# A one-core encoder layer: the residual's squares in the up product, the first v products on unscaled x, and other buffers for the last output pieces

## The chip, the cores and the metric

The kernel runs on one core of a Trainium2 chip. The core has five engines with queues of their own: TensorE (PE, matrix products into PSUM banks, with PEld its weight loads), VectorE (DVE), ScalarE (ACT), GpSimd (POOL) and SyncE (SP), which here issues the DMAs. An engine works through its queue in order; semaphores order the engines among each other.

The metric is the device time of one execution in microseconds (us); the median of several runs is given. One execution was also profiled: the profile has its own time and a span, from the first to the last instruction that it shows.

## The reference

One layer of an encoder on x of 2048 tokens by 1024 features, all in float32:

```
xn = rms_norm(x, mix_norm_g)
aq,ak,av,mq,mk,mv,mo,i,f,ga,gm = split(xn @ w_in)
A  = chunked band attention(aq, ak, av)      # own 64-token chunk and 8 before it
M  = gated recurrence with matrix memory(conv(mq), conv(mk), mv, i, f), normed, times sigmoid(mo)
y  = sigmoid(ga) * (A @ w_att_proj) + sigmoid(gm) * (M @ w_mlstm_proj)
x  = x + y @ w_out                           # the residual stream, called x2 below
x  = x + relu(rms_norm(x, ffn_norm_g) @ w_up)^2 @ w_down
out = rms_norm(x, final_norm_g)
rms_norm(x, g) = x * (mean(x*x over features) + 1e-6)^-0.5 * g
```

Since the norm's factor is one number per token, it can be applied to a product's rows after the product, where the token is the output's partition or column.

## The kernel before, in words

**Precision and tiles.** Each float32 operand is split into a high part (ACT, a cast) and a low part (DVE, source minus high); a product is three matmuls, high·high, high·low and low·high. `split_now` (L367, L369) does so for a weight tile of 128x1024, `split` (L703, or L705 with a scale, and L708, or L710) for a 128x512 tile of activations. Weight tiles come through four buffers `wraw` (512 KB loads) and three split buffers `wsp`. Activations lie feature by token: eight tiles k of 128 features by 512 tokens for a block of 512 tokens. Further pools: 28 split tiles `r`, 16 `ctx`, 6 `tmp`, 4 `sc` (mostly for reloads), 2 `bias`, and 8 PSUM banks.

**Stages.** Four blocks b of 512 tokens, in two halves s of two blocks. For each block: the norm (`norm_in`, `square_in`, `scale_in`), then with the split tiles `xs` the products v (`token_tiles`, L428 to L430), the i and f gates (L536), mv, then five feature tiles for each of four head groups, then ga, the attention and recurrence beside them, and the two projections. After two blocks, for the half as a whole: the gm product (2 quads), the out product (2), the up product (8) and the down product (8). A quad (`quad`, L511) is a 2x2 block product done with seven products, whose sums and differences DVE forms (`combine`, L1310; `spread`, L1364 to L1373; in the out product L1444).

**The first norm.** For block 0, `square_in` loads each x tile (L669), squares it on ACT (L675) and adds it up on DVE (L679). Products with ones (L633) give the mean by token, DVE and POOL (L644, the power −0.5) the factor `r_x`, PE broadcasts it (L652), `scale_in` multiplies x by gain and factor (L692), stores it and splits it into `xs`.

**The residual's squares.** When the out product has finished a tile of x2, `x2_tile` stores it to DRAM, multiplies it by the up norm's gain on ACT (L1471) and squares it on ACT (L1478, L1482); POOL adds the squares up (L1485) in the two `bias` buffers. `norm_mid` takes the sums by products with ones (L1506); its factor is only used later, in the down product.

**The end.** `final1` squares each finished tile (L1667), adds it up (L1670) and multiplies it by the last gain (L1674). `final_scale` takes the sums (L1684), POOL the power (L1693). `final_out` transposes on PE (L1702), scales on ACT (L1709) or DVE (L1711) into a `tmp` buffer and sends it out (L1715).

**Order.** Nothing is scheduled on the chip. Each part is a Python generator that says which engine it uses and for how long, in the author's estimate; `Flow` runs them against each other and writes each engine's instructions in the order that comes out. So a change anywhere can move instructions elsewhere, by the estimated times and by when buffers come free. `dense` is the main thread with all large products; it and its calls set PE's order.

Of the kernel before, what the change touches and what calls it, by code (L numbers as in the profile page):

```python
# [27 lines left out]
P = 128  # L28
# [17 lines left out]
N_Q = N_G + N_O + 2 * N_F  # L46

# [157 lines left out]
class Layer:  # L205
# [48 lines left out]
    def setup(self):  # L254
        nc, io = self.nc, self.io
        nc.vector.memset(self.half, -0.5)
        nc.vector.memset(self.ones, 1.0)
        yield "sp", 700
        nc.sync.dma_start(self.const, io["consts"].rearrange("p (a b) -> p a b", a=2))
        yield "sp", 50  # L260
        nc.sync.dma_start(self.gcol, io["gcol"].rearrange("p (a b) -> p a b", a=3))

    def setup_late(self):
        nc, io, fl = self.nc, self.io, self.fl
        (raw,) = yield "get", self.temp, 1
# [32 lines left out]
    def loader(self):  # L298
        fl, io = self.fl, self.io
        i = 0  # L300
        for s in range(NS):
            for n in range(2 * N_W):
                (raw,) = yield "get", self.wraw, 1
                fl.spawn(self.split_w(i, io["w"][n % N_W], raw), 0)
                i += 1
# [43 lines left out]
    def split_w(self, i, src, raw):  # L349
        yield "sp", 1750, 2000  # L350
        self.nc.sync.dma_start(raw, src)
        yield from self.split_now(i, raw)
# [165 lines left out]
    def dense(self):  # L518
        fl = self.fl
        none = [None] * KT  # L520
        for b in range(NB):
            s, B = b // 2, self.blk[b]
            xe = B["xn"]
# [5 lines left out]
            yield from self.token_tiles(xs, xe, lambda t, bk: self.evac_v(b, t, bk))  # L529
# [3 lines left out]
            for k in range(KT):  # L533
                yield "pe", 433
                for j in range(2):
                    self.nc.tensor.matmul(bk[:40], self.gw[:, k], xs[k][:, j],  # L536
                                          start=k == 0 and j == 0, stop=k == KT - 1 and j == 1)
            fl.spawn(self.gates(b, bk), 1)
            yield from self.token_tiles(xs, none, lambda t, bk: self.evac_mv(b, t, bk))
            self.banks.want = 2  # L540
            for j in range(4):
                for fn in (self.evac_q, self.evac_k, self.evac_conv_q, self.evac_conv_k, self.evac_og):
                    (bk,) = yield from self.feature_tile(xs, none)
# [32 lines left out]
            self.tots = yield "get", self.bias, 2  # L576
# [24 lines left out]
    def norm_in(self, b):  # L601
# [4 lines left out]
        if b == 0:  # L606
            (tot,) = yield "get", self.ctx, 1
            for k in range(KT):
                (x,) = yield "get", self.ctx, 1
                xt.append(x)  # L610
                fl.spawn(self.square_in(b, k, x, tot, ev), 0)
# [32 lines left out]
        nc.gpsimd.tensor_tensor(r, r, self.half, op=ALU.pow)  # L644
        if b % 2 == 1:
# [9 lines left out]
        for k in range(KT):  # L655
            (dst,) = yield "get", self.rpool, 1
            B["xs"].append(dst)
            if b > 0:
                (x,) = yield "get", self.sc, 1
                xt.append(x)  # L660
            fl.spawn(self.scale_in(b, k, xt[k], bk, dst, done[k]), 2)
        fl.set(B["xs_ev"])
# [3 lines left out]
    def square_in(self, b, k, x, tot, ev):  # L666
        fl, nc = self.fl, self.nc
        yield "sp", 900, 2000
        nc.sync.dma_start(x[:, :T], self.io["xt"][b, k])  # L669
        if k > 0:  # L670
# [12 lines left out]
    def scale_in(self, b, k, slot, bk, dst, ev):  # L683
# [12 lines left out]
        fl.set(self.blk[b]["xn"][k])  # L696
# [17 lines left out]
    def attention(self, b):  # L714
# [5 lines left out]
        B["kq"] = {}  # L720
        for j in range(4):
# [22 lines left out]
    def evac_v(self, b, t, bk):  # L744
# [4 lines left out]
        yield "act", act_ns(512, True)  # L749
        nc.scalar.copy(v[:, :, 0], src)  # L750
        yield "dve", dve_ns(512)
        nc.vector.tensor_sub(v[:, :, 1], src, v[:, :, 0].bitcast(F32))
# [201 lines left out]
    def gates(self, b, bk):  # L954
# [11 lines left out]
        yield "dve", 85  # L966
        V.tensor_add(self.gf, bk[:, :32].rearrange("p (a b) -> p a b", a=NT), self.bif)
# [103 lines left out]
    def evac_mv(self, b, t, bk):  # L1071
# [5 lines left out]
        yield "act", act_ns(512, True)  # L1077
        nc.scalar.copy(mv[:, :, 0:128], bk.rearrange("p (h c) -> p h c", h=MH))
# [384 lines left out]
    def x2_tile(self, s, h, j, x, ht, w, hev):  # L1463
# [10 lines left out]
        tot = self.tots[h][:, :512]  # L1474
        if not B["sums"]:
# [363 lines left out]
```

## Time and profile before

| | us |
|---|---|
| median of 3 runs (2904.01 to 2909.32) | 2906.3 |
| the profiled execution | 2907.77 |
| its span | 2906.0 |
| PE busy | 2853.2 (98%) |
| DVE busy | 2069.0 (71%) |
| ACT busy | 1562.5 (54%) |
| POOL busy | 98.4 (3%) |

PE's granted clock was 0.998 of full speed. The span divides, by PE's own lines, roughly into: the first half's blocks to 660 us, its gm and out products to 830, its up product to 1140, its down product to 1450, and the same for the second half, with the tail from 2890 on.

How to read it: a group or timeline row names the line of the code, the engine and the operation, output<-input by tile names without buffer numbers, and how many. In the timeline the first two numbers are start and length in us; what stands in brackets is how long the engine was idle before, and what ended that wait. PE is a matmul, PEld its weight load, SPq a DMA issue on SP's queue. A row of the waits says which engine and line waited for which, in total, how often, and the longest.

### The profile page before, as it was taken

What the parts mean: (1) busy time and instruction counts of PE and PEld (TensorE: products, weight loads), DVE (VectorE), ACT (ScalarE), POOL (GpSimd) and SP (SyncE); (2) the same over time, 40 slices, a digit from 0 to 9 for tenths busy, and PEclk for the clock granted to TensorE, in tenths of its full rate; (3) what the DMA queues carried; (4) which work ended last, traced back from release to release, by engine and by line L of the source; (5) the groups of instructions that cost most, each with busy time, mean ns of one, the idle gap of its engine ahead of it and who ended that gap; (6) DMA issues with size and microseconds to landing.
All of it is one profiled execution on the core that took longest, in us unless ns stands there. A gap on an engine that the chain in (4) does not pass through costs nothing.

```text
span 2906.0 us, 39057 instructions
## 1 busy us (share of the span) xinstructions
PE 2853.2 (98%) x13760; PEld 2381.8 (82%) x13760; DVE 2069.0 (71%) x3797; ACT 1562.5 (54%) x2708; POOL 98.4 (3%) x152
## 2 busy tenths in 40 slices
PE   7999999999999999999999999999999999999998
PEld 6888878888778888888888888888887788888887
DVE  5786569876885557898748864697769744468775
ACT  3664356654565556444536653566555655564444
POOL 0000000000110000000000000000001100000000
PEclk9999999999999999999999999999999999999999
DMA  5326942258875558766543246222588655587652
GB/s 200 101 91 235 331 143 94 73 180 282 276 246 212 210 203 290 255 227 209 203 157 105 87 130 212 97 82 68 176 290 288 221 200 186 191 288 232 201 183 88
DMA packets 232902, 548.07 MB, mean 189 GB/s; under 512 B 26240, under 2 KB 32512, under 8 KB 232704
## 3 DMA queue, kind: packets, MB, share of 16 engines
q1 hardware_dynamic: 232704, 545.57, 55.9%
q8 instruction: 108, 1.77, 0.2%
q14 instruction: 90, 0.74, 0.1%
HBM read 375.60 MB, written 169.87 MB: 188 GB/s over the span
## 4 chain that ended last, share of the span: by engine, by line
PE 58%; DVE 7%; DMA 4%; issue 2%; ACT 2%; SPq 0%; POOL 0%; POOLq 0%; DVEq 0%; ACTq 0%
PE bank L511 38%; PE bank L428 5%; PE bank L429 5%; PE bank L430 5%; DMA sc<-u 2%; DVE wsp L369 1%; DVE r L708 1%; PE bank L878 1%; PE bank L944 1%; PE bank L913 1%; DVE sc L919 1%; ACT wsp L367 0%; ACT r L703 0%; DMA sc<-hn 0%; DVE ctx L1108 0%
## 5 line engine op out<-in xcount | busy, mean ns | idle before, releaser
L511 PE MATMUL bank<-r,wsp 128*128 128x512 f32 x6720 | 1537.6, 390 | 15.2 <-DVE ctx L1444 5.4
L511 PEld LDWEIGHTS bank<-r,wsp 128*128 128x128 f32 x6720 | 1259.2, 188 | 283.3 <-ACT r L703 6.8
L369 DVE TENSOR_TENSOR wsp<-wraw,wsp 128x1024 fp32r<-128x1024 f32 x456 | 557.7, 1223 | 306.1 <-ACT wsp L367 301.8
L367 ACT CAST wsp<-wraw 128x1024 fp32r<-128x1024 f32 x456 | 478.9, 1050 | 534.6 <-PE bank L511 295.4
L428 PE MATMUL bank<-r,wsp 128*128 128x512 f32 x1152 | 463.3, 402 | 3.4 <-DVE tmp L890 2.0
L430 PE MATMUL bank<-r,wsp 128*128 128x512 f32 x1152 | 450.2, 391 | 0.0
L429 PE MATMUL bank<-r,wsp 128*128 128x512 f32 x1152 | 449.8, 390 | 0.0
L703 ACT CAST r<-sc 128x512 fp32r<-128x512 f32 x276 | 170.0, 621 | 162.7 <-DMA sc<-u 71.3
L430 PEld LDWEIGHTS bank<-r,wsp 128*128 128x128 f32 x1152 | 216.2, 188 | 47.0
L428 PEld LDWEIGHTS bank<-r,wsp 128*128 128x128 f32 x1152 | 216.9, 188 | 42.5 <-DVE tmp L890 2.8
L429 PEld LDWEIGHTS bank<-r,wsp 128*128 128x128 f32 x1152 | 217.1, 188 | 36.7
L708 DVE TENSOR_TENSOR r<-sc,r 128x512 fp32r<-128x512 f32 x276 | 187.8, 700 | 58.9 <-ACT r L703 58.3
L1619 DVE TENSOR_TENSOR ctx<-bank,ctx 128x512 f32<-128x512 f32 x192 | 132.1, 689 | 73.6 <-PE bank L511 73.3
L1310 DVE TENSOR_TENSOR ctx<-bank,ctx 128x512 f32<-128x512 f32 x120 | 82.7, 689 | 85.6 <-PE bank L511 85.6
L928 ACT ACTIVATE sc<-sc,scs 128x640 f32<-128x640 f32 (+4 forms) x128 | 97.3, 761 | 82.3 <-DVE scs L925 78.3
L919 DVE CUSTOM_DVE_ANT_0 sc<-bank,bias 128x320 f32<-128x320 f32 (+3 forms) x240 | 103.1, 462 | 18.8 <-PE bank L913 18.1
L878 PEld LDWEIGHTS bank<-r,r 128*128 128x128 f32 x672 | 98.3, 189 | 12.4 <-DVE r L949 2.9
L878 PE MATMUL bank<-r,r 128*128 128x256 f32 (+1 forms) x672 | 105.5, 279 | 1.9 <-DVE r L949 1.2
L1554 ACT ACTIVATE ctx<-ctx 128x512 f32<-128x512 f32 x96 | 60.6, 632 | 85.5 <-DVE ctx L1310 85.4
L428 PE MATMUL bank<-wsp,r 128*128 128x512 f32 x256 | 102.5, 400 | 1.5 <-ACT r L703 1.5
L429 PE MATMUL bank<-wsp,r 128*128 128x512 f32 x256 | 100.5, 393 | 0.0
L430 PE MATMUL bank<-wsp,r 128*128 128x512 f32 x256 | 99.4, 391 | 0.0
(214 smaller groups left out, 2925.7 us busy)
## 6 DMA issues: line engine op xcount, KB each, us to landing
wraw<-in_w SPq DMA_DIRECT2D x176, 512.0 KB, 3.5
wraw<-in_wf SPq DMA_DIRECT2D x136, 512.0 KB, 4.3
sc<-u SPq DMA_DIRECT2D x224, 256.0 KB, 3.6
wraw<-wsum SPq DMA_DIRECT2D x96, 512.0 KB, 3.9
wsum<-wraw SPq DMA_DIRECT2D x64, 512.0 KB, 2.9
u<-ctx SPq DMA_DIRECT2D x128, 256.0 KB, 2.4
u<-tmp SPq DMA_DIRECT2D x96, 256.0 KB, 2.7
tmp<-proj SPq DMA_DIRECT2D x64, 256.0 KB, 4.5
```

The source lines that it names most:

```text
L367: nc.scalar.copy(w[:, 0], raw)
L369: nc.vector.tensor_sub(w[:, 1], raw, w[:, 0].bitcast(F32))
L428: mm(ps, lh, rh, start=first, stop=False)
L429: mm(ps, lh, rl, start=False, stop=False)
L430: mm(ps, ll, rh, start=False, stop=last)
L511: mm(ps, wv[:, x, k, n], a[:, y], start=new and k == 0 and x == y == 0, stop=k == 3 and x == 1, skip_group_check=True)
L703: self.nc.scalar.copy(dst[:, 0], src)
L708: self.nc.vector.tensor_sub(dst[:, 1], src, dst[:, 0].bitcast(F32))
L878: nc.tensor.matmul(bk[:, c0:c0 + w], st, sl[:, x, o:o + w], start=n == 0, stop=n == total - 1)
L919: nc.vector.tensor_tensor_reduce(out=e[:, x * w:x * w + w], in0=bks[x][:, :w], in1=br[:, j0 + x * w:j0 + x * w + w], op0=ALU.add, op1=ALU. ...
L928: nc.scalar.activation(e[:, :n], e[:, :n], AF.Exp, scale=-1.0, bias=mx, accum_out=st[:, 2:3])
L1619: nc.vector.tensor_add(a, ps, a)
```

## The change

1. **First block.** `square_in` now also multiplies each x tile by the gain alone and splits it (lines 695 and 697 of the changed file: ACT the high part, DVE the low), into eight tiles `xg`. v, the gates and mv of block 0 are taken from `xg`; the factor `r_x` is applied where their banks are emptied: `evac_v`, `evac_mv` by the scale operand, `gates` in four rows with the bias. `xs` (with the factor) is still made, for the other feature tiles. The DMAs are put in a written order: gcol, then x tiles and weight tiles in turn, then the constants, the last x tiles, and the small loads.
2. **Squares of x2.** `x2_tile` no longer squares. `norm_mid` is started with the third quad of the up product (and `norm_in` of the next block with it); it loads x2 again into `sc` buffers, squares on ACT and adds on DVE, in the new function `square_mid`.
3. **The end.** In the second half, the square of the last tile (3, 1) isn't added up: it is multiplied by ones in products of its own, into the bank that holds the others' sums. The output pieces of the last block go into `sc` and `wraw` buffers in place of `tmp`.

The core of the diff:

```diff
+LAST = (3, 1)
 def setup(self):
-        yield "sp", 700
-        nc.sync.dma_start(self.const, ...)
         yield "sp", 50
         nc.sync.dma_start(self.gcol, ...)
+        self.fl.set(self.ev_gain)
+        yield "wait", [self.w_sent[2]]
+        yield "sp", 700, 2000
+        nc.sync.dma_start(self.const, ...)
+        self.fl.set(self.ev_const)
 def setup_late(self):
+        yield "wait", [self.x_sent[6], self.ev_const]
 def loader(self):
+                first = s == 0 and n < KT // 2
+                if first:
+                    yield "wait", [self.x_sent[2 * n]]
...
 def dense(self):
             xs = B["xs"]
-            yield from self.token_tiles(xs, xe, ...evac_v...)
+            vs = xs if b > 0 else B["xg"]
+            yield from self.token_tiles(vs, B["xn"], ...evac_v...)
...
-            yield from self.token_tiles(xs, none, ...evac_mv...)
+            yield from self.token_tiles(vs, none, ...evac_mv...)
+            if b == 0:
+                fl.put(self.rpool, *vs)
...
-            self.tots = yield "get", self.bias, 2
...
-            for h in range(2):
-                fl.spawn(self.norm_mid(s, h), 2)
-            if b + 1 < NB:
-                fl.spawn(self.norm_in(b + 1), 3)
             for i in range(N_F):
+                if i == 2:
+                    for h in range(2):
+                        fl.spawn(self.norm_mid(s, h), 3)
+                    if b + 1 < NB:
+                        fl.spawn(self.norm_in(b + 1), 3)
 def square_in(self, b, k, x, tot, ev):
+        dst, g = self.blk[b]["xg"][k], self.gcol[:, 0, k:k + 1]
+        if k > 0:
+            yield "wait", [self.w_sent[(k - 1) // 2]]
         nc.sync.dma_start(x[:, :T], self.io["xt"][b, k])
+        fl.set(self.x_sent[k])
+        yield "wait", [self.ev_gain]
+        nc.scalar.mul(dst[:, 0], x[:, :T], g)
+        nc.vector.scalar_tensor_tensor(dst[:, 1], x[:, :T], g, dst[:, 0].bitcast(F32), op0=ALU.mult,
+                                       op1=ALU.subtract)
+        fl.set(self.blk[b]["xn"][k])
 def evac_v(self, b, t, bk):
+        if b == 0:
+            r = self.rr["x"][:, t:t + 1]
+            yield "wait", [self.ev_r]
+            nc.scalar.mul(v[:, :, 0], src, r)
+            nc.vector.scalar_tensor_tensor(v[:, :, 1], src, r, v[:, :, 0].bitcast(F32), ...)
...
 def x2_tile(...):
-        tot = self.tots[h][:, :512]
-        if not B["sums"]:
-            nc.scalar.square(tot, x5)
-        else:
-            nc.scalar.square(sq[:, :512], x5)
-            nc.gpsimd.tensor_tensor(tot, tot, sq[:, :512], op=ALU.add)
 def norm_mid(self, s, h):
+        for j in range(KT):
+            (x,) = yield "get", self.sc, 1
+            fl.spawn(self.square_mid(s, h, j, x, tot[:, :512], summed), 3)
+        yield "wait", summed
...
+    def square_mid(self, s, h, j, x, tot, summed):
+        x5 = x[0][:, :512]
+        yield "sp", 900, 2000
+        self.nc.sync.dma_start(x5, self.x2d[2 * s + h].ap()[j])
+        yield "act", act_ns(512)
+        self.nc.scalar.square(tot if j == 0 else x5, x5)
+        if j > 0:
+            yield "wait", [summed[j - 1]]
+            yield "dve", dve_ns(512)
+            self.nc.vector.tensor_add(tot, tot, x5)
+        self.fl.put(self.sc, x)
+        self.fl.set(summed[j])
 def final1(...):
+        if s == NS - 1 and (j, h) == LAST:
+            (self.sq_last,) = yield "get", self.temp, 1
+            nc.scalar.square(self.sq_last[:, :512], a)
+            fl.set(self.last_ev)
+            nc.scalar.mul(a, a, self.gcol[:, 2, j:j + 1])
+            return
 def final_scale(...):
+        if last:
+            yield "wait", [self.last_ev]
+            for t in range(NT):
+                nc.tensor.matmul(bk[:, 2 * t:2 * t + 2], self.sq_last[:, t * P:(t + 1) * P], self.ones,
+                                 start=False, stop=True, skip_group_check=True)
 def final_out(...):
+        pool = self.temp
+        if s == NS - 1 and h == LAST[1]:
+            pool = (self.sc, self.wraw)[g]
```

More of the change, by code (lines that the diff above doesn't have):

```diff
@@ L347, in load_w, with split_w @@
         self.fl.set(ev)
-    def split_w(self, i, src, raw):
+    def split_w(self, i, src, raw, sent=None):
         yield "sp", 1750, 2000
         self.nc.sync.dma_start(raw, src)
+        if sent is not None:
+            self.fl.set(sent)
         yield from self.split_now(i, raw)
@@ L528, in dense @@
             xs = B["xs"]
-            yield from self.token_tiles(xs, xe, lambda t, bk: self.evac_v(b, t, bk))
+            vs = xs if b > 0 else B["xg"]
+            yield from self.token_tiles(vs, B["xn"], lambda t, bk: self.evac_v(b, t, bk))
             yield "wait", [self.ev_late]
@@ L720, in attention @@
         B["kq"] = {}
+        if b == 0:
+            yield "wait", [self.ev_late]
         for j in range(4):
@@ L965, in gates @@
                              start=True, stop=True)
-        yield "dve", 85
-        V.tensor_add(self.gf, bk[:, :32].rearrange("p (a b) -> p a b", a=NT), self.bif)
+        if b == 0:
+            for c in range(NT):
+                yield "dve", 85
+                V.scalar_tensor_tensor(self.gf[:, c], bk[:, c * 8:c * 8 + 8], self.rr["x"][:, c:c + 1],
+                                       self.bif[:, c], op0=ALU.mult, op1=ALU.add)
+        else:
+            yield "dve", 85
+            V.tensor_add(self.gf, bk[:, :32].rearrange("p (a b) -> p a b", a=NT), self.bif)
         fl.put(self.temp, tmp)
@@ L1680, in final_scale @@
         (bk,) = yield "get", self.banks, 1
-        yield "wait", summed
+        last = s == NS - 1 and h == LAST[1]
+        yield "wait", [e for j, e in enumerate(summed) if not last or j != LAST[0]]
         yield "pe", 900
```

84 lines of the change are left out of this document (50 added, 34 removed).

## The prediction

> **What bounds the kernel now.** I read the page's busy line and chain first, then who made TensorE (PE) wait, then the timeline at the places where it waited.
>
> ```profile
> PE 2853.2 (98%) x13760; PEld 2381.8 (82%) x13760; DVE 2069.0 (71%) x3797; ACT 1562.5 (54%) x2708; POOL 98.4 (3%) x152
> PE 58%; DVE 7%; DMA 4%; issue 2%; ACT 2%; SPq 0%; POOL 0%; POOLq 0%; DVEq 0%; ACTq 0%
> ```
>
> PE is busy 2853.2 of 2906.0 us, so 52.8 us are idle. The change takes no product away, so all it can win lies in those 52.8 us. The waits of PE, longest first:
>
> ```profile
> PE bank L633 <- DVE ctx L679: 11.3, 1, 11.3
> PE bank L511 <- DVE ctx L1444: 5.4, 3, 2.1
> PE bank L511 <- ACT r L705: 3.7, 2, 1.9
> ...
> PE bank L652 <- POOL r_x L644: 2.3, 1, 2.3
> ...
> PE bank L511 <- DVE r L708: 1.3, 1, 1.3
> ...
> PE bank L1506 <- POOL bias L1485: 1.1, 2, 0.8
> ```
>
> The columns are total, times and longest, in us. Three places carry them: the first block's norm (L633, L652) at the start, the out product and its neighbours (L1444, L705, L708, L1485), and the tail. The change touches all three. In the built program's order of instructions PE, DVE and ACT differ from before only around these places; elsewhere their rows follow each other as they did, so I take the other waits (attention, the down product) as unchanged.
>
> **Part 1, the start.** The timeline of before (start, length, engine, line):
>
> ```profile
> 0.73 1.28 ACT L675 ACT_TABLE_LOAD   x1 [0.73 <-PEq L1829]
> ...
> 0.73 3.71 SPq L669 DMA_DIRECT2D ctx<-in_xt  x8
> ...
> 3.45 0.63 ACT L675 ACTIVATE ctx<-ctx 128x512 f32<-128x512 f32 x1 [1.44 <-DMA ctx<-in_xt]
> ...
> 5.88 3.34 ACT L675 ACTIVATE tmp<-ctx 128x512 f32<-128x512 f32 x5 [1.09 <-DMA ctx<-in_xt]
> ...
> 11.06 1.04 ACT L367 CAST wsp<-wraw 128x1024 fp32r<-128x1024 f32 x1 [1.04 <-DMA wraw<-in_w]
> ...
> 13.25 1.23 DVE L369 TENSOR_TENSOR wsp<-wraw,wsp 128x1024 fp32r<-128x1024 f32 x1
> 13.41 1.94 POOL L644 TENSOR_TENSOR r_x<-r_x,half 128x4 f32<-128x4 f32 x1 [12.48 <-DVE r_x L640]
> ...
> 15.41 2.07 PE L652 MATMUL bank<-const,r_x 128*128 128x128 f32 x8 [2.27 <-POOL r_x L644]
> ...
> 18.97 0.80 PE L428 MATMUL bank<-wsp,r 128*128 128x512 f32 x1 [1.49 <-ACT r L703]
> ...
> 825.26 0.95 PE L1506 MATMUL bank<-ones,bias 128*128 128x2 f32 x8
> ...
> 2894.54 0.72 ACT L1674 ACTIVATE ctx<-ctx,gcol 128x512 f32<-128x512 f32 x1
> ```
>
> The first product starts at 18.97, after eight x tiles, the sum of squares, the power on POOL, the broadcast on PE, and a scaled split. Changed, its inputs are one x tile times the gain, and one weight tile. I walk the new chain:
> - SP issues one DMA per 3.71/8 = 0.46 us. gcol now stands first, so x tile 0, which was ready at 3.45, comes at about 3.9.
> - In the built program ACT waits for that tile's DMA ahead of its table load, because the wait became an instruction of its own. The load, hidden at 0.73 before, ends at 3.9 + 1.28 = 5.2.
> - The gain product (0.72, the L1674 row) ends at 5.9, the tile's square (0.63) at 6.5.
> - Weight tile 0 is now second in the queue. Tiles x0 to x2 are as many bytes as x0 and this weight tile; they were in at 5.88. With gcol ahead that is 6.3, so ACT is the later one. Its high half (1.04) ends at 7.6.
>
> So the first product starts at 7.65, 11.3 us earlier. Three things come off. PE issues two products and then needs the weight's low half on DVE (1.23 behind 7.6, so 8.9), a wait of 0.4. The norm's sixteen PE rows, which ran before the first product, now stand inside the stream; the L1506 row gives 0.95 for eight at full clock, some 1.3 for all beyond what overlaps. The slow first products (0.80 for the first) are paid in both. Start: 11.3 − 0.4 − 1.3 = 9.6.
>
> What must hide behind the stream: the norm chain, moved and not removed. The last x tile is now issued behind five weight tiles and five small loads. Eight x tiles came from 3.45 to 9.2, 0.8 us each, so with the bytes of 17 tiles ahead it lands at 3.9 + 17 × 0.8 = 17.5 or a little later; its split stands behind that of a weight tile on ACT and DVE, and I place it at 25. It is needed when the fourth weight tile starts, three tiles of 24 products (0.22 each by the stage row of part 2) and the slow start after 8, at 26. The power (1.94) then has some 7 us of PE work before the broadcast asks for it. Scaling and splitting eight tiles moves beside the first block's mv product, 96 products or 21 us long, with DVE nearly full there. The gate recurrence stands behind these eight tiles on DVE, and PE's small products on it may wait 0 to 0.5 us. The scalings in evac_v, evac_mv and gates replace copies one for one, four gate rows replace one, all behind PE's stream. On SP the eight xn stores wait for the later scaling and two weight tiles stand behind some of them; these are used three query or key tiles later, so I cost that at nothing, and at a wait of some 2 us if the scaling slips. Bounds: 11.3 − 1.3 = 10 with no wait for the low half, and 8.2 if the table load costs all of 0.73 to 3.45 (see the rivals). I take 9.6.
>
> **Part 2, the squares of the residual stream.**
>
> ```profile
> 754.62 2.00 POOL L1485 TENSOR_TENSOR bias<-bias,tmp 128x512 f32<-128x512 f32 x1 [166.35 <-ACT tmp L1482]
> 756.65 0.69 DVE L1364 TENSOR_TENSOR tmp<-ctx,ctx 128x512 f32<-128x512 f32 x1 [1.18 <-POOL bias L1485]
> ...
> 758.06 2.53 PE L511 MATMUL bank<-r,wsp 128*128 128x512 f32 x8 [1.77 <-ACT r L705]
> ...
> 816.61 2.98 PE L511 MATMUL bank<-r,wsp 128*128 128x512 f32 x12 [1.78 <-DVE ctx L1444]
> 821.04 4.38 PE L511 MATMUL bank<-r,wsp 128*128 128x512 f32 x18 [1.45 <-DVE ctx L1444]
> ...
> 825.54 1.77 DVE L1364 TENSOR_TENSOR tmp<-ctx,ctx 128x512 f32<-128x512 f32 x1
> ...
> 842.57 3.74 PE L511 MATMUL bank<-r,wsp 128*128 128x512 f32 x15 [1.28 <-DVE r L708]
> ...
> 2204.47 2.41 DVE L710 SCALAR_TENSOR_TENSOR r<-tmp,r 128x512 fp32r<-128x512 f32 x2
> 2205.04 1.29 POOL L1485 TENSOR_TENSOR bias<-bias,tmp 128x512 f32<-128x512 f32 x1 [160.79 <-ACT tmp L1482]
> ...
> 2208.19 4.18 PE L511 MATMUL bank<-r,wsp 128*128 128x512 f32 x17 [1.89 <-ACT r L705]
> ...
> 2265.54 7.18 PE L511 MATMUL bank<-r,wsp 128*128 128x512 f32 x30 [2.15 <-DVE ctx L1444]
> ```
>
> ```profile
> L1485 POOL TENSOR_TENSOR bias<-bias,tmp x28: 1285/1444/1998, 754.6 to 2277.8; 128x512 f32<-128x512 f32 x28
> 880.00:920.00 40.00, 40.00 (x182) 33.29 (x181) 22.37 (x26) 20.80 (x30) 1.97 (x1) 1.00 0.63 222
> sc<-u SPq DMA_DIRECT2D x224, 256.0 KB, 3.6
> ```
>
> (The first line is one source line's instructions, min/median/max in ns. The second is a stage: length, then busy PE, PEld, DVE, ACT, POOL, the clock, DMA share, GB/s. The third is from the page's DMA issues.)
>
> These rows show more than POOL's own wait. While POOL adds, DVE stands still: L1364 takes 0.69 at 756.65 and 1.77 at 825.54, two L710 take 2.41 where two take some 1.3, and at 756.65 DVE is held 1.18 until POOL ends. So each of the 28 adds costs DVE some 1.1 us where DVE is what PE waits for. Removed: 28 POOL adds, and 32 ACT squares (0.63) that stood between the ACT splits. What comes back:
> - First half. At 758.06, 1.18 of 1.77. At 816.61, 821.04 and 842.57, with 0.3 of L1485's 1.1, at most 1.78 + 1.45 + 1.28 + 0.3 = 4.8 and at least nothing, since DVE has a full queue of its own there. Six or more adds lie in it, 6.6 us of DVE time, more than the waits, but PE asks earlier by what it wins. I take two thirds, 3.2.
> - Second half. At 2208.19, 1.1 of 1.89. At 2265.54 and for the other 0.8 of L1485, 2.0 of 2.95.
>
> That is 1.2 + 3.2 + 1.1 + 2.0 = 7.5.
>
> Added, from the third up quad on: 32 reloads of x2 (SP issues of 0.46, so 15 us of a queue over two up products, and 8 MB where the DMA share is 0.63), 32 ACT squares (the same work, later) and 28 DVE adds of 0.69. One half's 14 adds are 9.7 us of DVE, and the seven sums of the next block's norm_in (4.8), which ran before, move in with them: 14.5 against 40 − 22.4 = 17.6 free. It fits with little left. Behind an add that waits for its square stand the weight splits (L369), and behind those PE. At best it costs nothing or even helps, as norm_in leaves the crowded 840 to 850. At worst one wait like the longest L1444 (2.1) in each half, 4.2. I take 0.5 a half. Part 2: 7.5 − 1.0 = 6.5, with ends 2.5 and 9.5.
>
> **Part 3, the tail.**
>
> ```profile
> 2894.54 0.69 DVE L1670 TENSOR_TENSOR bias<-bias,tmp 128x512 f32<-128x512 f32 x1 [0.70 <-ACT tmp L1667]
> ...
> 2897.66 1.84 ACT L1709 ACTIVATE tmp<-bank,r_z 128x512 f32<-128x512 f32 x3 [2.40 <-POOL r_z L1693]
> ...
> 2898.38 4.45 SPq L1715 DMA_DIRECT2D out_x<-tmp  x8
> 2900.53 1.37 ACT L1709 ACTIVATE tmp<-bank,r_z 128x512 f32<-128x512 f32 x2 [1.03 <-DMA out_x<-tmp]
> ```
>
> The last square is multiplied by ones directly, without the add of 2894.54 (0.73 with its hand-over); the four extra PE products for the other seven run earlier, beside the last product. The last eight pieces go to weight and sc buffers, so ACT's 1.03 wait for a sent piece goes. What is late next is SP: eight issues that took 4.45 can follow each other in 3.71. Gain 0.73 + 0.74 = 1.47, at least 0.7 if they don't pack; I take 1.4.
>
> **Sum.** 9.6 + 6.5 + 1.4 = 17.5. The span goes from 2906.0 to 2888.5. The profiled execution took 2907.77, 1.5 above the median of 2906.3, so it goes to 2890.3 and the median to about 2889.
>
> **A page against the sum.** The rows do not say what the table load costs when its wait is on the path: ACT's next work, at 3.45, waited for a DMA. It costs between 1.28 and 3.45 − 0.73 = 2.72. At 2.72 the start gives 8.2, and the time is 2890.2. I take 1.28, since the page names DMA and nothing of ACT for the rest. The Trainium skill, page "ScalarE: Activation LUTs", section "What ACT_TABLE_LOAD costs", puts a drain of some 1.38 us on top of a load of 1.28; by that rule the case of 2890.2 holds. No run here shows the drain.
>
> **Rivals.**
> - The load costs 2.72 (above): 2890.2, chance 0.14.
> - Part 2 wins nothing: DVE was full by its own work, and the new adds cost what POOL's gave. For it: the 842.57 wait is behind a full DVE queue. Against: the 1.18 held by POOL. 2906.3 − 9.6 − 1.4 = 2895.3, chance 0.17.
> - The norm chain returns as a wait: PE stands at the broadcast or at the first query product for the scaled tiles. It would give back most of the start, some 8 us: 2897. For it: DVE is crowded from 37 to 56 us. Against: 22 us of cover. Chance 0.08.
> - Slower: the new adds stand at the head of DVE's queue waiting for reloads. A reload takes 3.6 to land, and with 0.6 and 0.7 for square and add a round of four sc buffers takes 4.9; eight rounds are 39 us. If the weight splits wait through them, less 16 us that three split weight tiles cover (24 products each, 5.3 us), PE loses 23 and the time is about 2912. It decides when an add holds DVE more than 17.5/28 = 0.6 us longer than it runs. Against: each stage of 40 us has room. Chance 0.05.
>
> The forecast has 0.56; alone it reaches from 2884 to 2894. With the second and third rival the range is 2882 to 2898. A measurement here can tell about 0.2%, 5.8 us, from no change. Faster (under 2900.5): 0.56 + 0.14 + 0.16 + 0.06 = 0.92; slower 0.04; the same 0.04.
>
> **What would show it.** Start: the first product near 7.7 us with the table load at about 3.9, no wait over 1 us on PE from 9 to 75 us. Part 2: no L1485-like POOL rows, DVE tensor rows of 0.69 throughout the out product, PE waits between 740 and 850 of some 4 us and not 8, in the second half below 2; none over 1 us in the up product. Tail: 6.8 us from the end of the last square to the end of the last issue, where it was 8.3 (2894.54 to 2902.83). Wrong would be a first product past 10, a PE wait at the broadcast of r_x, or waits on weight splits beside the new adds.

## The result and the profile after

| | before | after |
|---|---|---|
| median, us | 2908.89 (6 runs, 2904.01 to 2909.94) | 2894.65 (6 runs, 2892.78 to 2899.16) |
| ratio, 95% interval | 1 | 0.9956 [0.9943, 0.9969] |
| profiled execution, us | 2907.77 | 2896.59 |
| its span, us | 2906.0 | 2894.7 |

The ratio is a gain of 12.8 us (9.0 to 16.6) where 17.5 was forecast; the median of 2894.65 lies 5.7 above the 2889 forecast and inside the range of 2882 to 2898. (The forecast counts from 2906.3, the median of the first three runs of before; with three more it is 2908.89.) Lines of the code moved: the first products are now L438 to L440 (L428 to L430 before), the others L521 (L511), the loads, scalings and sums as named below.

The busy line of the page after, and its list of what PE waited for (total, times, longest, us):

```profile
PE 2853.5 (99%) x13768; PEld 2381.7 (82%) x13768; DVE 2073.6 (72%) x3836; ACT 1566.7 (54%) x2715; POOL 55.4 (2%) x124
```

```profile
PE bank L438 <- ACT wsp L377: 7.5, 1, 7.5
PE bank L521 <- DVE ctx L1361: 4.4, 4, 2.1
PE bank L521 <- DVE r L738: 2.9, 2, 1.9
...
PE bank L521 <- DVE r L740: 1.9, 2, 1.1
...
PE bank L521 <- ACT r L733: 1.8, 1, 1.8
```

PE does the same work (2853.5 for 2853.2), and is idle 41.2 us instead of 52.8. The three waits of the first norm (11.3, 2.3, 1.5) are one of 7.5; the sums of the out product (L1444, now L1495) and POOL are gone from the list. The gate and up products' sums (L1361, before L1310) have grown from 1.1 to 4.4.

**The start.** The timeline of after:

```profile
3.93 1.28 ACT L695 ACT_TABLE_LOAD   x1 [3.93 <-DMA ctx<-in_xt]
...
5.22 0.72 ACT L695 ACTIVATE r<-ctx,gcol 128x512 fp32r<-128x512 f32 x1
...
6.37 1.03 ACT L377 CAST wsp<-wraw 128x1024 fp32r<-128x1024 f32 x1
...
7.45 1.22 PE L438 MATMUL bank<-wsp,r 128*128 128x512 f32 x2 [7.45 <-ACT wsp L377]
8.71 0.29 PEld L439 LDWEIGHTS bank<-wsp,r 128*128 128x128 f32 x1 [0.76 <-DVE wsp L379]
...
30.41 0.95 PE L647 MATMUL bank<-ones,ctx 128*128 128x2 f32 x8
...
38.19 1.05 PE L669 MATMUL bank<-const,r_x 128*128 128x128 f32 x8
...
233.32 0.49 PE L1224 MATMUL bank<-ctx,ctx 128*128 128x129 f32 x2 [1.92 <-DVE ctx L1212]
```

The first product starts at 7.45, and the order and the times of the chain are those forecast to 0.2 us (3.9, 5.2, 5.9, 6.5, 7.6; here 3.93, 5.21, 5.94, 6.46, 7.40). It is 11.5 us earlier than 18.97. At the wait in the attention, which both kernels have, it is still 8.9 earlier. Its row of before:

```profile
242.20 0.49 PE L1173 MATMUL bank<-ctx,ctx 128*128 128x129 f32 x2 [2.14 <-DVE ctx L1161]
```

**The squares.** The waits of PE in after, in the places that the prediction listed, and one that is new:

```profile
747.19 77.59 PE L521 MATMUL bank<-r,wsp 128*128 128x512 f32 x339 [1.12 <-DVE r L740]
825.71 55.97 PE L521 MATMUL bank<-r,wsp 128*128 128x512 f32 x244 [0.94 <-DVE r L738]
883.75 16.41 PE L521 MATMUL bank<-r,wsp 128*128 128x512 f32 x71 [2.07 <-DVE ctx L1361]
...
2271.61 28.69 PE L521 MATMUL bank<-r,wsp 128*128 128x512 f32 x116 [1.95 <-DVE r L738]
```

The waits of 758.06, 816.61, 821.04 and 831.45 have no counterpart. At 725.27, in the gm product, PE waits 1.72 us where before waits 0.44 (at 732.86). The wait of 883.75 stands in the up product, where the new reloads and the next block's norm now run. To have one number for all of part 2 I take the four stretches 700 to 800, 800 to 950, 2120 to 2240 and 2240 to 2330 (460 us, the gate, out and the first up products of both halves) and subtract PE's busy time. The sums of that view, before and then after:

```profile
sum 460.00, PE 446.82 PEld 365.62 DVE 356.99 ACT 266.84 POOL 42.48; mean PE 111.71 PEld 91.41 DVE 89.25 ACT 66.71 POOL 10.62
```

```profile
sum 460.00, PE 450.80 PEld 368.29 DVE 352.05 ACT 269.85 POOL 0.00; mean PE 112.70 PEld 92.07 DVE 88.01 ACT 67.46 POOL 0.00
```

PE is idle 13.2 us there before and 9.2 after. (Products at a lowered clock count as busy in this number.)

**The tail.** First before, then after:

```profile
2890.80 2.32 PE L511 MATMUL bank<-r,wsp 128*128 128x512 f32 x9
...
2895.29 1.05 PE L1684 MATMUL bank<-ones,bias 128*128 128x2 f32 x8 [0.84 <-DVE bias L1670]
```

```profile
2878.86 1.64 PE L521 MATMUL bank<-r,wsp 128*128 128x512 f32 x6
2880.34 0.95 PE L1750 MATMUL bank<-ones,bias 128*128 128x2 f32 x8
2881.14 0.96 PE L521 MATMUL bank<-r,wsp 128*128 128x512 f32 x3
...
2882.86 0.63 ACT L1719 ACTIVATE tmp<-ctx 128x512 f32<-128x512 f32 x1 [4.03 <-DVE ctx L1675]
...
2883.55 1.05 PE L1757 MATMUL bank<-ones,tmp 128*128 128x2 f32 x8
...
2886.63 0.33 SPq L1791 DMA_DIRECT2D out_x<-wraw  x1
...
2890.49 0.60 SPq L1791 DMA_DIRECT2D out_x<-wraw  x1
```

The add is gone and ACT waits for no piece, but from the start of the last nine products to the end of the last issue it is 12.03 us before (2890.80 to 2902.83) and 12.23 after (2878.86 to 2891.09). The last product ends 2.32 us into this stretch before and 3.24 us into it after, with the rows of 2880.34 in between.

### The profile page after: what moved, and what is told of

Same layout as the page of the kernel before. It is cut to its first block, busy times and chain, and to the rows that moved or that the text cites. A ratio compares the mean times of both kernels' runs of the same rounds, so it can differ in the third digit from the quotient of the medians.

```text
span 2894.7 us, 39100 instructions
## 1 busy us (share of the span) xinstructions
PE 2853.5 (99%) x13768; PEld 2381.7 (82%) x13768; DVE 2073.6 (72%) x3836; ACT 1566.7 (54%) x2715; POOL 55.4 (2%) x124
## 3 DMA queue, kind: packets, MB, share of 16 engines
q8 instruction: 108, 1.77, 0.3%
## 4 chain that ended last, share of the span: by engine, by line
PE 76%; DVE 12%; DMA 5%; ACT 4%; issue 3%; SPq 0%; POOL 0%; DVEq 0%; POOLq 0%; ACTq 0%
PE bank L521 40%; PE bank L438 10%; PE bank L439 10%; PE bank L440 9%; DVE wsp L379 2%; PE bank L919 2%; DMA sc<-u 1%; PE bank L985 1%; PE bank L954 1%; DVE r L738 1%; ACT wsp L377 1%; DVE sc L960 1%; DVE ctx L1159 1%; DMA sc<-y 1%; DMA ctx<-in_xt 1%
## 5 line engine op out<-in xcount | busy, mean ns | idle before, releaser
L521 PE MATMUL bank<-r,wsp 128*128 128x512 f32 x6720 | 1538.1, 390 | 12.8 <-DVE ctx L1361 4.4
L521 PEld LDWEIGHTS bank<-r,wsp 128*128 128x128 f32 x6720 | 1258.8, 188 | 281.2 <-DVE ctx L1361 9.0
L438 PE MATMUL bank<-r,wsp 128*128 128x512 f32 x1152 | 464.3, 403 | 3.3 <-DVE tmp L931 1.9
L440 PE MATMUL bank<-r,wsp 128*128 128x512 f32 x1152 | 450.8, 391 | 0.0
L440 PEld LDWEIGHTS bank<-r,wsp 128*128 128x128 f32 x1152 | 216.7, 188 | 47.2
L438 PEld LDWEIGHTS bank<-r,wsp 128*128 128x128 f32 x1152 | 217.2, 189 | 42.5 <-DVE tmp L931 2.7
L1361 DVE TENSOR_TENSOR ctx<-bank,ctx 128x512 f32<-128x512 f32 x120 | 82.5, 688 | 75.4 <-PE bank L521 75.4
L438 PE MATMUL bank<-wsp,r 128*128 128x512 f32 x256 | 102.2, 400 | 7.5 <-ACT wsp L377 7.5
L440 PE MATMUL bank<-wsp,r 128*128 128x512 f32 x256 | 100.4, 393 | 0.0
```

The lines of the kernel that those rows point to most:

```text
L438: mm(ps, lh, rh, start=first, stop=False)
L440: mm(ps, ll, rh, start=False, stop=last)
L521: mm(ps, wv[:, x, k, n], a[:, y], start=new and k == 0 and x == y == 0, stop=k == 3 and x == 1, skip_group_check=True)
```

## The experiments

Each ran beside the kernel before on the same chip; the gain is 2907 us times one less the ratio. "Idle" is PE's idle time in the four stretches.

| kernel | ratio, 95% interval | gain, us | idle, us |
|---|---|---|---|
| start_only | 0.9963 [0.9951, 0.9976] | 10.8 | 13.0 |
| squares_only | 0.9982 [0.9973, 0.9991] | 5.2 | 8.5 |
| tail_only | 0.9996 [0.9987, 1.0005] | 1.2 | 14.0 |
| table_early | 0.9948 [0.9936, 0.9961] | 15.1 | 9.5 |
| add_on_dve | 0.9966 [0.9954, 0.9978] | 9.9 | 6.3 |
| no_add | 0.9956 [0.9944, 0.9968] | 12.8 | 7.3 |
| no_mid | 0.9941 [0.9929, 0.9953] | 17.2 | 5.7 |
| two_queues | 0.9950 [0.9938, 0.9962] | 14.5 | 7.6 |
| start_dve | 0.9941 [0.9928, 0.9953] | 17.2 | 7.3 |
| best | 0.9934 [0.9920, 0.9947] | 19.2 | 4.8 |
| norm_apart | 0.9951 [0.9939, 0.9964] | 14.2 | 8.5 |
| after_again | 0.9947 [0.9934, 0.9959] | 15.4 | 7.8 |

An interval is 2.6 to 4 us to either side. The idle column is one execution each, but falls into groups that do not overlap: 13.0 to 14.0 with POOL's adds, 7.6 to 9.5 with part 2, 4.8 to 7.3 with the sums on DVE in the out product. The two kernels that leave sums out stand at 7.3 (no_add) and 5.7 (no_mid).

**The three parts alone.** Theory: the prediction's terms 9.6, 6.5 and 1.4. Rival: the shifts read off the two traces, 8.9, some 3 and about nothing.

Part 1 alone (the edits of `setup`, `norm_in`, `square_in`, `dense`, `gates`, the evictions and the loader):

```diff
+            vs = xs if b > 0 else B["xg"]
+            yield from self.token_tiles(vs, B["xn"], lambda t, bk: self.evac_v(b, t, bk))
...
+        nc.scalar.mul(dst[:, 0], x[:, :T], g)
...
+            nc.scalar.mul(v[:, :, 0], src, r)
```

> The kernel before with part 1 alone (v products of the first block on x without the norm's scale, norm chain moved into the stream); squares and tail as before. By the prediction's terms it is 9.6 us faster than before. By the shifts read off the two traces (first product 11.5 us earlier, 8.9 us left at 98 us and still 8.85 at 550 us) it is 8.9 us faster. If the norm chain came back as a wait somewhere later (rival), under 4 us.

Part 2 alone:

```diff
-            yield "pool", 1150
-            nc.gpsimd.tensor_tensor(tot, tot, sq[:, :512], op=ALU.add)
...
+                if i == 2:
+                    for h in range(2):
+                        fl.spawn(self.norm_mid(s, h), 3)
...
+    def square_mid(self, s, h, j, x, tot, summed):
```

> The kernel before with part 2 alone (squares of the residual stream in the up product, from reloads, summed on VectorE). By the prediction's terms it is 6.5 us faster than before. By the shifts in the trace of after (3.7 us in the first half, 0.95 lost again around 1286 to 1455, 0.4 in the second half) it is about 3.2 us faster. Rival: VectorE was full of its own work and part 2 wins nothing: 0. If the granted clock fell by chance after one 1.95 us wait in the profiled run of after, the second half here loses no clock and the gain is nearer 5.

Part 3 alone:

```diff
+        if s == NS - 1 and (j, h) == LAST:
+            (self.sq_last,) = yield "get", self.temp, 1
...
+            pool = (self.sc, self.wraw)[g]
```

> The kernel before with part 3 alone (last square multiplied by ones directly, last eight output pieces in weight and sc buffers). By the prediction's terms it is 1.4 us faster than before. Rival, from the trace of after: the eight rows of the extra ones products (0.95 us) stand in PE's stream ahead of the last three groups of products, and the eight last SP issues take 4.46 us as they did (4.45), so it is between 0 and 0.6 us slower.

Measured: 10.8 (7.0 to 14.2), 5.2 (2.6 to 7.8) and 1.2 (from 1.5 slower to 3.8 faster). The sum of 17.2 is not told from 12.8 by these intervals. The times do not decide between the two values of the start. For the tail the traces decide: from the start of the last nine products of the down product to the end of the last issue it is 11.90 to 12.04 us in the seven profiles with the tail of before, and 12.23 or 12.24 in the six with part 3 and all issues on SP. Part 3 costs 0.2 to 0.3 us there. To the end of the span it is 15.2 to 15.6 and 15.4 to 16.2 us, so nothing is won behind the last issue either. In tail_only the ones products stand in the stream as in after:

```profile
2890.65 1.64 PE L512 MATMUL bank<-r,wsp 128*128 128x512 f32 x6
2892.13 0.95 PE L1695 MATMUL bank<-ones,bias 128*128 128x2 f32 x8
2892.93 0.95 PE L512 MATMUL bank<-r,wsp 128*128 128x512 f32 x3
```

**The table load.** One activation that depends on nothing but a constant, at the head of ACT's queue of after:

```diff
         nc.vector.memset(self.ones, 1.0)
+        nc.scalar.square(self.mid[0], self.half)
```

> The kernel after with one small square of a constant tile at the start of ACT's queue, so that the activation table is loaded from 0.8 us on and not behind the first x tile. If the load of 1.28 us is all that it costs on the path, ACT's first product of x with the gain starts at about 3.95 instead of 5.22, and the first matmul product at 6.2 instead of 7.45, if weight tile 0 has landed by 5.1: 1.2 us faster than after. Rival: weight tile 0 lands only at about 6.3, then the first product stays at 7.4 and nothing is won. If a drain of some 1.4 us came on top of the load, a gain of 2.5 us would show.

```profile
0.73 1.28 ACT L259 ACT_TABLE_LOAD   x1 [0.73 <-PEq L1907]
2.02 0.20 ACT L259 ACTIVATE mid<-half 128x4 f32<-128x4 f32 x1
3.87 0.72 ACT L696 ACTIVATE r<-ctx,gcol 128x512 fp32r<-128x512 f32 x1 [1.64 <-DMA ctx<-in_xt]
...
5.78 1.04 ACT L378 CAST wsp<-wraw 128x1024 fp32r<-128x1024 f32 x1 [0.67 <-DMA wraw<-in_w]
```

```profile
6.87 1.22 PE L439 MATMUL bank<-wsp,r 128*128 128x512 f32 x2 [6.87 <-ACT wsp L378]
```

The load is back at 0.73 and the first activation starts 1.35 us earlier (3.87 for 5.22). The first product starts only 0.58 earlier, since ACT now waits 0.67 for weight tile 0 (the row of 5.78). So the load cost 0.58 us of the 1.28 in after; behind it stood the weight's DMA, and the answer lies between the two expectations. The first activation behind the load starts 0.01 us after the load's end here (2.01 to 2.02), and as in after (5.21 to 5.22). As a time the step can't be measured: 15.1 for 12.8 with intervals of 3.7.

**Who held DVE.** The kernel before, with the adds of the out product given to DVE in their place:

```diff
-            yield "pool", 1150
-            nc.gpsimd.tensor_tensor(tot, tot, sq[:, :512], op=ALU.add)
+            yield "dve", dve_ns(512)
+            nc.vector.tensor_add(tot, tot, sq[:, :512])
```

> The kernel before with the 28 sums of squares in the out product on VectorE (DVE) in place of GpSimd (POOL); the 32 squares on ACT stay where they are. If a POOL add holds up DVE for its own length (the prediction's mechanism, some 1.1 us each), DVE has 28 times 0.69 us instead of 28 times 1.1 us, so the rows of 1.77 us go back to 0.69, PE's waits in the out product (13.2 us from 700 to 950 and 2120 to 2330 in before) fall by some 2 us, and the kernel is 1 to 3 us faster. If POOL and DVE do not hold each other up and DVE was merely full, 19 us more on DVE make the waits longer and the kernel 2 to 5 us slower.

And with the adds left out (only the two POOL lines removed, so that the second norm's sum lacks all but one tile):

> The kernel before without the 28 POOL sums in the out product: the sum of squares holds the first tile of each half alone, so the second norm's value is not computed. The 32 squares on ACT stay. If POOL's adds are what part 2 wins by, this wins what part 2 alone wins (5 us) or a little more, and the two waits of 1.8 and 1.5 us on the out product's sums at 816 and 821 us go. If the squares on ACT were the cause, it wins at most the 1.1 us that PE waited for POOL's last add.

Measured: 9.9 us faster (6.4 to 13.4) and 12.8 (9.3 to 16.3), far more than either theory gave. Three groups of DVE's instructions from 740 to 860, by shape (busy us, mean ns), in before and then in add_on_dve:

```profile
L708 DVE TENSOR_TENSOR r<-sc,r 128x512 fp32r<-128x512 f32 x14 | 10.9, 795 | 4.4 <-ACT r L703 4.4
L708 DVE TENSOR_TENSOR r<-ctx,r 128x512 fp32r<-128x512 f32 x8 | 7.3, 930 | 1.6 <-ACT r L703 1.6
L1373 DVE TENSOR_TENSOR ctx<-ctx,ctx 128x512 f32<-128x512 f32 x6 | 6.3, 1048 | 0.0
```

```profile
L708 DVE TENSOR_TENSOR r<-sc,r 128x512 fp32r<-128x512 f32 x14 | 9.6, 688 | 5.0 <-ACT r L703 5.0
L708 DVE TENSOR_TENSOR r<-ctx,r 128x512 fp32r<-128x512 f32 x8 | 5.3, 687 | 0.4 <-ACT r L703 0.4
...
L1373 DVE TENSOR_TENSOR ctx<-ctx,ctx 128x512 f32<-128x512 f32 x6 | 4.1, 688 | 0.0
```

The same instructions take 0.69 each where no POOL add runs, and up to 1.05 on average where they do. The squares on ACT are in both new kernels, so they were not the cause. That POOL's adds lengthen DVE's instructions, and that PE's waits shrink when the adds leave POOL, is shown.

How the one leads to the other is not simply DVE's time. The six groups of this view that are longer in before lose 8.2 us together, over 14 adds, which is 0.6 us an add; an add on DVE itself takes 0.69. In the four stretches DVE is busy 357.0 us in before and 356.6 in add_on_dve, with the 28 adds in it, and PE still waits half as long (6.3 for 13.2). So DVE's time in all does not explain the gain; likely it matters when DVE is held, which is not shown. One candidate is the planner: it lays out the instructions knowing of an add on DVE but not of one on POOL that blocks DVE. Another is a buffer: the squares that POOL reads lie in `tmp` buffers, of which there are six. At 756.65 DVE's instruction writes such a buffer, and it is POOL's add, ending at 756.62, that releases it after 1.18 us of waiting; ACT's split of its output starts at 757.38 and PE at 758.06, after the wait of 1.77. There no DVE instruction was lengthened: the buffer was late. No run separates these ways.

**What the new work costs.** The kernel after, with 28 of the 32 reloads and squares and all 28 adds left out (the second norm's sum lacks them):

```diff
-        for j in range(KT):
-            (x,) = yield "get", self.sc, 1
-            fl.spawn(self.square_mid(s, h, j, x, tot[:, :512], summed), 3)
-        yield "wait", summed
+        (x,) = yield "get", self.sc, 1
+        fl.spawn(self.square_mid(s, h, 0, x, tot[:, :512], summed), 3)
+        yield "wait", summed[:1]
```

> The kernel after with the reload, square and add of 28 of the 32 residual tiles left out of the up product (the second norm's value is not computed; one tile of each half is still squared). The prediction put the new work at 0.5 us a half: 1.0 us faster than after. If the new adds cost nothing, the same as after. If they are what the 2.07 us wait at 883.75 comes from, that wait goes and the kernel is 2 us or more faster than after.

Its sum over the four stretches:

```profile
sum 460.00, PE 454.26 PEld 372.27 DVE 339.86 ACT 261.59 POOL 0.00; mean PE 113.56 PEld 93.07 DVE 84.97 ACT 65.40 POOL 0.00
```

17.2 us faster than before (13.7 to 20.6), with 5.7 us idle. So taking the squares and adds out of the out product wins 13.4 (the mean of before, start_only and tail_only) less 5.7 = 7.7, and the six kernels with the whole of part 2 (mean 8.5) give 2.8 of it back. The 5.7 is one execution; the six spread by 1.9. The new waits are in the up product: about 883 in the first half, of 1.1 to 2.1 us in squares_only, after, table_early, two_queues and after_again, and about 2290 in the second, of 0.6 to 1.95 in all of these but the first profile of after. In before, start_only, tail_only, no_mid, no_add, add_on_dve, start_dve and best PE waits at neither place. Over the six kernels the two waits average 1.3 and 1.1 us, 2.3 of the 2.8.

The next run starts the next block's norm ahead of the up product again, as before:

```diff
+            if b + 1 < NB:
+                fl.spawn(self.norm_in(b + 1), 3)
             for i in range(N_F):
                 if i == 2:
                     for h in range(2):
                         fl.spawn(self.norm_mid(s, h), 3)
-                    if b + 1 < NB:
-                        fl.spawn(self.norm_in(b + 1), 3)
```

> The kernel after, with the next block's norm (its reloads, squares and adds) started ahead of the up product as in the kernel before; only the residual squares wait for the third up quad. If the wait of 1.4 to 2.1 us that the kernels with part 2 show in the up product of the first half (883.75 in after) comes from the two chains of adds together, it goes, and the kernel is 1 to 2 us faster than after, with the waits between 840 and 850 back. If the residual squares alone make it, it stays, as the second half (1.3 to 1.95 us at about 2290, with no next block's norm) speaks for.

The wait of 883 goes, 0.55 at 844 comes, 1.02 at 2287 stays, and the wait of 747.19 (1.12 in after) is 2.26. In the first half it was the next block's norm; in after the adds of DVE in front of it are those of L640, the norm's:

```profile
881.27 0.69 DVE L640 TENSOR_TENSOR sc<-sc,sc 128x512 f32<-128x512 f32 x1 [0.19 <-ACT sc L637]
881.88 1.22 DVE L400 TENSOR_TENSOR wraw<-wraw,wraw 128x1024 f32<-128x1024 f32 x1
883.01 0.69 DVE L1361 TENSOR_TENSOR ctx<-bank,ctx 128x512 f32<-128x512 f32 x1
```

In the second half, which has no next norm, it is the residual squares: in norm_apart an add of theirs at 2284.23 and a weight split at 2284.83 stand on DVE ahead of the sum of 2285.97 that PE waits for. The time does not move (14.2 for 12.8 and 15.4).

**The last pieces.** The kernel of table_early with three of the last eight pieces issued by ACT:

```diff
+SPLIT = ((2, 1), (3, 0), (3, 1))
...
+        if s == NS - 1 and h == LAST[1] and (t, g) in SPLIT:
+            yield "act", 100, 2000
+            nc.scalar.dma_start(self.io["out"][row:row + P, g * 512:g * 512 + 512], o[:, :512])
```

> The kernel after with the table load at the start (as in the run before) and three of the last eight output pieces issued from ACT's queue instead of SP's. If SP's eight issues of 4.45 us in all are what the tail waits for, the last issue ends 1.2 us earlier (five on SP end 2.5 us after the first, three on ACT 1.5 us after ACT's last piece): 1.2 us faster than with the table load alone, about 16 us faster than before. If what is late is the landing of the pieces (3.2 to 3.6 us after the last issue), nothing is won.

The last issue now ends 6.55 us after the last square (2877.34 to 2883.89) instead of 7.61 in table_early, but the span ends 5.2 us after it instead of 3.7: nothing is won. The DMA view of after over its last 14 us (40 slices of 0.35 us) says why:

```profile
GB/s 0 0 0 0 0 0 0 0 0 0 0 0 0 0 0 0 0 0 0 240 380 369 404 375 398 375 380 375 380 375 392 375 386 381 375 35 0 0 0 0
DMA packets 1152, 2.10 MB, mean 150 GB/s; under 512 B 128, under 2 KB 128, under 8 KB 1152
```

Eight pieces are 2.1 MB, and from the first byte to the last they move at some 380 GB/s, which takes 5.5 us. In two_queues the rate is the same (357 to 404), and in before too (357 to 421), where the pieces lie in `tmp` buffers. Neither the buffers, which part 3 changed, nor SP's issues set this end.

**A better version.** Part 1, the table load at the start, the sums in the out product on DVE, the tail as before; and the same without the table load. Against start_only:

```diff
+        nc.scalar.square(self.mid[0], self.half)
...
-            yield "pool", 1150
-            nc.gpsimd.tensor_tensor(tot, tot, sq[:, :512], op=ALU.add)
+            yield "dve", dve_ns(512)
+            nc.vector.tensor_add(tot, tot, sq[:, :512])
```

The last of the three is the changed kernel again, unedited, for the comparison.

> Part 1 as in the kernel after, with the table load at the start; the squares of the residual stream stay in the out product, but are summed on VectorE (DVE) in place of GpSimd (POOL); the tail as in the kernel before. If the measured gains add up (10.8 for the start, 9.9 for the sums on DVE, some 0.6 to 1.0 for the table load), it is about 21 us faster than before, 8 us faster than after. If the start's gain and the sums' overlap, for instance because run to run slow clock after a wait made up part of either, 15 to 17 us.

> The same without the early table load: part 1, and the sums in the out product on DVE. By adding up: 20.7 us faster than before. Beside the run before it tells what the table load costs: its wait was 0.58 us at the first product (6.87 instead of 7.45).

> The changed kernel once more, beside the three others on the same chip: 12.8 us faster than before (9.0 to 16.6). Its profile shows whether the two places of lowered clock (234 and 2272 us, some 1.7 us each) stand again; if the place is chance, one of them or both are elsewhere or missing.

best is 19.2 us faster than before (15.4 to 23.3), at a median of 2888.08 (2886.9 to 2890.3). after_again, on the same chip, has 2890.64 (2889.82 to 2896.08). best has the lowest median of all kernels that compute the whole, and its four stretches are idle 4.8 us instead of 7.6 to 9.5; but the intervals of the two ratios overlap, so that it beats after is likely and not shown. start_dve stands at 17.2, between the two. Whether the gains add up isn't decided: 20.7 (10.8 and 9.9) lies just inside the interval of start_dve (13.7 to 20.9), and 21 inside that of best.

## Why the prediction was right or wrong

- **The start, 9.6.** Right in mechanism: 8.9 by the trace of after, 10.8 (7.0 to 14.2) by time. The first product came at 7.45 for 7.65 forecast, with the load at 3.93 as forecast; PE has no wait at all from 9 to 88 us, so the norm chain is hidden. Of the 11.5 us, 2.6 are lost again, where 1.7 were forecast. The wait for the low half costs PE the 0.4 forecast (the 0.76 in the row of 8.71 is idle time of the weight load, not of PE). The norm's two groups of rows (30.41 and 38.19) push back the products behind them by 0.9 us each, 1.8 in place of 1.3. And the slow first products are not "paid in both" alike: some 0.43 us apart and not 0.23, they go on for two products more in after. From the first product to the twelfth it is 4.17 us in before (18.97 to 23.14) and 5.03 in after (7.45 to 12.48): 0.4 is the wait, and the other 0.45 these two.
- **The table load as a rival.** The case of 2.72 is refuted: 0.01 us lie between load and activation. The step was also too dear at 1.28, as the weight tile came only some 0.6 us before ACT was free.
- **Squares, what is won: 7.5.** The number is right: 7.7 by no_mid. That POOL's adds cause it is shown by add_on_dve and no_add. The price is not: "some 1.1 us" of DVE for each add was that of the rows picked, where all groups give 0.6, and 28 adds put on DVE at 0.69 each left most of the gain. So the way from the adds to PE's waits was argued through DVE's time, which does not explain it; beyond the one place at 758.06 it stays open. The waits from the gm product to 850 sum to 3.8 after (725.27 to 825.71) for 8.3 before (732.86 to 842.57), as forecast ("some 4 us and not 8").
- **Squares, what is paid: "I take 0.5 a half".** This is the step that failed most: 2.8 and not 1.0. "It fits with little left" counted DVE's free time in the stage. PE waited all the same, about 883 and 2290, because the norm's and the residual's adds came ahead of a sum that PE needed. The 2.8 lies between the 1.0 taken and its own worst case of 4.2, nearer to the latter. The forecast "none over 1 us in the up product" was wrong (2.07), and so was "in the second half below 2" (3.2 at 2172.90 to 2271.61). The net of 6.5 is 4.9 (13.4 less 8.5).
- **The tail, 1.4.** Wrong in sign by 0.2. The four extra products were costed at nothing "beside the last product". PE is the engine that everything waits for there, so their eight rows from 2880.34 on make the last product end 0.92 us later (3.24 for 2.32), more than the 0.73 of the skipped add. That SP would pack its issues into 3.71 took 0.46 an issue from the start of the kernel; here eight take 4.45 before and 4.46 after, and behind them the bytes set the end. The forecast 6.8 from last square to last issue is 7.6.
- **The sum.** 8.9 + 4.9 − 0.2 = 13.6, against 12.8 (9.0 to 16.6) and 15.4 (11.9 to 19.2) in two sets of runs. The rival "part 2 wins nothing" is refuted by squares_only (2.6 to 7.8), that of the norm chain by the trace. Of the slower rival, adds at the head of DVE's queue, a milder form exists: adds ahead of a sum, and not of weight splits that wait through reloads, at about an eighth of the 23 us that it was given. That the time lies inside the range owes something to luck: 2894.65 is just above the 2884 to 2894 of the forecast alone, in the part that was added for the two refuted rivals. Counted from its own 2906.3, the gain of 12.8 gives 2893.5, at the upper end of the forecast's own reach.

## What to carry to other kernels

That GpSimd is idle does not make an elementwise instruction on it free: here it held up DVE instructions that read two SBUF tiles, and 28 of these adds given to DVE in place won about as much as moving the work away promised, without reloads. Free time of an engine over a stage does not tell whether a new instruction lands in front of the one that the bound engine waits for; until a trace says otherwise, price it nearer to the longest such wait than to nothing. At the end of a kernel, look first at the bytes still to move, then at queues and buffers.

## What was not expected of the hardware

**A wait can cost more than its length.** The granted clock of PE, in stretches of 2 us (length, then busy PE, PEld, DVE, ACT, POOL, the clock, DMA share, GB/s), behind the wait of 233.32 and behind that of 2271.61 in after:

```profile
234.00:236.00 2.00, 2.00 (x8) 1.63 (x7) 1.74 (x4) 1.46 (x4) 0.00 (x0) 0.51 0.80 282
236.00:238.00 2.00, 2.00 (x9) 1.61 (x8) 1.02 (x3) 0.65 (x4) 0.00 (x0) 0.63 0.96 249
2272.00:2274.00 2.00, 2.00 (x6) 1.56 (x5) 2.00 (x4) 1.66 (x4) 0.00 (x0) 0.50 0.01 3
2274.00:2276.00 2.00, 2.00 (x7) 1.57 (x7) 2.00 (x4) 1.19 (x2) 0.00 (x0) 0.70 0.90 288
```

The first loses 2 × 0.49 + 2 × 0.37 = 1.7 us and the second 1.6, on top of waits of 1.92 and 1.95. The same wait in after_again:

```profile
234.26 0.49 PE L1224 MATMUL bank<-ctx,ctx 128*128 128x129 f32 x2 [2.04 <-DVE ctx L1212]
```

```profile
234.00:236.00 2.00, 1.74 (x11) 1.56 (x12) 1.64 (x4) 1.00 (x2) 0.00 (x0) 1.00 0.71 240
```

It is longer and costs nothing more. So whether a wait of some 2 us is followed by a slow clock differs from execution to execution. This wait, of 1.75 to 2.15 us, stands in all fourteen profiles, and the clock falls behind it in nine. The profile of before has such a place elsewhere, behind the wait of 758.06, which has no counterpart in after (its lowest stretch; from 758 to 764 it loses 1.7 us):

```profile
760.00:762.00 2.00, 2.00 (x6) 1.60 (x5) 2.00 (x4) 0.42 (x1) 0.00 (x0) 0.50 0.85 245
```

The two places in after account for 3.3 of the 5.9 us between the profiled spans of after (2894.7) and after_again (2888.8), the same kernel; this is a part of why single executions differ by 6 us and why the time of a small step can't be read from one. The Trainium skill, page "TensorE: Matmul & The Clock Gate", section "Part 1: The HAM clock gate (the "warmup" mystery)", has a free-running window of about 3.4 us behind such a change of clock, which would fit that equal waits differ; it asks for one idle window of that length, and the trace does not agree: 1.92 us of waiting was enough, and 1.77 in before.

**What a POOL add blocks.** In before, POOL adds from 815.55 to 817.00. Of DVE's rows beside it

```profile
815.78 0.68 DVE L1444 TENSOR_TENSOR ctx<-bank,ctx 128x512 f32<-128x512 f32 x1
816.38 1.70 DVE L390 TENSOR_TENSOR wraw<-wraw,wraw 128x1024 f32<-128x1024 f32 x1
```

the one that reads a PSUM bank takes its 0.68, the one with two SBUF inputs 1.70 instead of 1.22 (its mean in add_on_dve). The Trainium skill, page "SBUF — State Buffer", section "SBUF: two separate sides", says that a DVE instruction with two SBUF inputs and a GpSimd one that reads SBUF exclude each other for the whole instruction; the trace agrees.
